# Splitting feed-forward weights into two parts with casting and adding DMAs instead of ScalarE and VectorE

## The chip, the cores and the metric

The kernel runs on one core of a Trainium2 chip. The time is the device time of one execution in microseconds (us); the figure quoted for a kernel is the median of its runs. The kernel before took 936.67 us (3 runs, 936.47 to 938.75). Engines are named as in the profile: PE is TensorE's matmul, PEld its weight load, DVE is VectorE, ACT is ScalarE, POOL is GpSimd, SP is SyncE, which here only issues DMAs.

## What is computed

One decoder layer on x of 512 tokens by 1024 columns in float32. Three token mixers (a gated recurrence, a differential attention and a forgetting attention) are merged and added to x; then comes the feed-forward part, which the change touches:

```python
h = rmsnorm(x, norm2_g[l])
u = causal_dwconv(h @ ffn_up[l], ffn_conv_w[l], ffn_conv_b[l])   # ffn_up: 1024 x 5632
u_gate, u_val = jnp.split(u, 2, axis=-1)
x = x + (jax.nn.gelu(u_gate) * u_val) @ ffn_down[l]              # ffn_down: 2816 x 1024
return rmsnorm(x, final_g)
```

## The kernel before

Every large matmul is made of three: each float32 operand is split into a high part of type float32r and a low part, operand minus high part, and the products high x high, high x low and low x high are summed in PSUM.

A weight block is 128 x 1024 numbers, 512 KB. `load_w` (L93) fetches one: SP issues a DMA into a tile `wr` (L100), ACT casts `wr` into the high tile `wh` (L101), DVE subtracts and writes the low tile `wl` (L102). `wr`, `wh` and `wl` have three buffers each, in rotation: a block's tiles are those of the block three before. `load_wp` (L105) does the same into four half-size tiles of another pool (`wph`, `wpl`).

The feed-forward part has two stages. In the up stage 44 blocks of `ffn_up` are used in turn, one item each: 24 matmuls of 512 columns into one PSUM bank (`up`, L912), 16 that read `wh` and then 8 that read `wl`. The first three items are done together in halves of 256 columns (`up_half`, L917), block 0 from `load_wp`, blocks 1 and 2 from `load_w`. After each second item `glu` (L921) runs the convolution and the gate on ACT and DVE and leaves `acth` and `actl`. The down stage does the 512 columns of either half of the output (`hf` 0 and 1) one after the other: 11 blocks each, 24 matmuls a block into four banks `psd` (`dmm`, L971), in which `wh` and `wl` alternate. The last 2 (`hf` 0) and 4 (`hf` 1) blocks of a half come from `load_wp` and are "held": all of a bank's matmuls are then done bank by bank. For `hf` 0 the blocks before these are called d0 to d8 here, for `hf` 1 e0 to e6.

The order on each engine is not written out by hand: a scheduler orders the instructions by its own simulated times and by which buffers are free. Each engine then works through its list in order; whatever waits on a semaphore holds all that stands behind it on that engine.

Of the kernel before, what the change touches and what calls it, by code (L numbers as in the profile page):

```python
# [10 lines left out]
F32 = mybir.dt.float32  # L11
F32R = mybir.dt.float32r
AF = mybir.ActivationFunctionType
ALU = mybir.AluOpType
ADD, SUB, MUL, MAX = ALU.add, ALU.subtract, ALU.mult, ALU.max
# [6 lines left out]
NF = DFF // 128  # L22
# [5 lines left out]
WCOL = 1088  # L28
# [18 lines left out]
def build(ctx, tc, A, out):  # L47
    nc = tc.nc
    PE, V, SC, G = nc.tensor, nc.vector, nc.scalar, nc.gpsimd
# [3 lines left out]
    wpool = ctx.enter_context(tc.tile_pool(name="wpool", bufs=3))  # L53
# [7 lines left out]
    def pg(name, dt=F32):  # L61
        return page.tile([128, 512], dt, name=name, tag="pg")
# [4 lines left out]
    def bank(name):  # L67
        return psm.tile([128, 512], F32, name=name, tag="mm")

    def abank(name):  # L70
        return psa.tile([128, 512], F32, name=name, tag="at")
# [4 lines left out]
    def mm(ps, a, b, start, stop):  # L76
        PE.matmul(ps, a, b, start=start, stop=stop)  # L77

    def mm3(ps, pairs, late=0):


        hh = [((ah, bh), (ah, bl), (al, bh)) for ah, al, bh, bl in pairs]
        if late == 2:
            seq = [m for t in hh for m in t]
        else:
            seq = [t[i] for t in hh for i in ((0, 1) if late == 0 else (0, 2))]
            seq += [t[2 if late == 0 else 1] for t in hh]
        for j, (a, b) in enumerate(seq):
            mm(ps, a, b, j == 0, j == len(seq) - 1)
# [3 lines left out]
    def load_w(ap, n, parts=1):  # L93
        raw = wpool.tile([128, WCOL], F32, name="wr", tag="wr")
        hi = wpool.tile([128, WCOL], F32R, name="wh", tag="wh", bufs=3)
        lo = wpool.tile([128, WCOL], F32R, name="wl", tag="wl", bufs=3)
        with tc.high_priority() if hp[0] else ExitStack():
            for p in range(parts):
                c = slice(n // parts * p, n // parts * (p + 1))
                nc.sync.dma_start(raw[:, c], ap[:, c])  # L100
                SC.copy(hi[:, c], raw[:, c])  # L101
                V.tensor_sub(lo[:, c], raw[:, c], hi[:, c])  # L102
        return hi, lo

    def load_wp(ap):  # L105

        raw = wpool.tile([128, WCOL], F32, name="wr", tag="wr")
        nc.sync.dma_start(raw[:, :1024], ap)
        res = []
        for p in range(2):  # L110
            c = slice(512 * p, 512 * (p + 1))
            h = pg("wph", F32R)
            l = pg("wpl", F32R)
            SC.copy(h, raw[:, c])
            V.tensor_sub(l, raw[:, c], h)
            res.append((h, l))
        return res
# [72 lines left out]
    for w in range(KD // 2):  # L190
        load_x(2 * w)
        hi, lo = load_w(A["wv_d"][w], 1024, 2)
        load_x(2 * w + 1)
        if w == 0:
            nc.sync.dma_start(cols[:, 8:], A["cols"][:, 8:])
        todo = [(t, 2 * w + kk, j) for kk in range(2) for j in range(3) for t in range(NT)]
        if w == KD // 2 - 1:
            todo.sort()
        for t, k, j in todo:
            kk = k % 2  # L200
            a, b = ((xh[k], hi), (xl[k], hi), (xh[k], lo))[j]
            mm(pst[t], a[:, 128 * t:128 * (t + 1)], b[:, 512 * kk:512 * (kk + 1)],
               k == 0 and j == 0, k == KD - 1 and j == 2)

    ss1 = const.tile([128, 2, NT], F32, name="ss1")
    for t in range(NT):
        for hf in range(2):
            xt = ag("xt")
            nc.sync.dma_start(xt, A["x"][128 * t:128 * (t + 1), 512 * hf:512 * (hf + 1)])
            SC.activation(xt, xt, AF.Square, accum_out=ss1[:, hf, t:t + 1])  # L210
    pre_w = [load_w(A["w_t"][i], 1024) for i in (T_DQ, T_DK)]
    ssum = small([128, NT], "ssum", 1)
    V.tensor_add(ssum, ss1[:, 0, :], ss1[:, 1, :])
# [47 lines left out]
    def vload_t(ap, kper, n):  # L261
        return lambda: [load_w(ap[0], kper * n), load_w(ap[1], kper * n)]
# [582 lines left out]
        hp[0] = True  # L845
    hp[0] = False

    def up_w(idx, paged=False):
        if paged:
            pp = load_wp(A["up_t"][idx])  # L850
            return lambda k: tuple(x[:, 128 * (k % 4):128 * (k % 4 + 1)] for x in pp[k // 4])
        hi, lo = load_w(A["up_t"][idx], 1024)
        return lambda k: (hi[:, 128 * k:128 * (k + 1)], lo[:, 128 * k:128 * (k + 1)])

    first_w = {0: up_w(0, True)}
    x1 = []
    x1p = [[pg("x1") for _ in range(2)] for _ in range(NT)]
# [12 lines left out]
    for t in range(NT):  # L870
# [3 lines left out]
        for hf in range(2):  # L874
            ps = bank("pswo")
# [36 lines left out]
    def up(wt, name):  # L912
        ps = bank(name)
        mm3(ps, [wt(k) + (h2h[k], h2l[k]) for k in range(KD)])
        return ps

    def up_half(ps, wt, hf):  # L917
        c = slice(256 * hf, 256 * (hf + 1))
        mm3(ps[:, c], [wt(k) + (h2h[k][:, c], h2l[k][:, c]) for k in range(KD)])

    def glu(c, psg, psv):  # L921
        ug = conv(psg, [col("fw", 44 * j + c) for j in range(3)], col("fb", c))
        uv = conv(psv, [fwh[:, 22 * j + c:22 * j + c + 1] for j in range(3)], fwh[:, 66 + c:67 + c])
        q = pg("gq")
        SC.activation(q, ug, AF.Square)
        V.tensor_scalar(q, q, GELU_A, 1.0, op0=MUL, op1=ADD)
        V.tensor_mul(q, q, ug)
        SC.activation(q, q, AF.Tanh, scale=GELU_C)  # L928
        V.scalar_tensor_tensor(ug, q, 1.0, ug, op0=ADD, op1=MUL)  # L929
        V.tensor_mul(ug, ug, uv)  # L930
        acts.append(split(ug, "act", ag if c < 10 else None))

    acts = []
    order = [i for c in range(NF) for i in (c, NF + c)]
    first_w[1] = up_w(order[1])
    first_w[2] = up_w(order[2])
    pss = [bank("psu") for _ in range(3)]
    for hf in range(2):
        for n in range(3):
            up_half(pss[n], first_w[n], hf)  # L940
    nxt = up_w(order[3])
    glu(0, pss[0], pss[1])
    prev = pss[2]
    for n in range(3, 2 * NF):
        w, nxt = nxt, up_w(order[n + 1]) if n + 1 < 2 * NF else None
        ps = up(w, "psu")
        if n % 2:
            glu(n // 2, prev, ps)
        prev = ps

    ss3 = const.tile([128, NT, 2], F32, name="ss3")
    NP = NF // 2
# [6 lines left out]
    def finish(t):  # L959
        z = rsqrt_act(ss3[:, t, 1:2], ss3[:, t, 0:1], "rs3")  # L960
        o = [pg("of") for _ in range(2)]
        SC.activation(o[1], x1[t][1], AF.Copy, scale=z)
        V.tensor_scalar(o[0], x1[t][0], z, None, op0=MUL)
        nc.sync.dma_start(out[128 * t:128 * (t + 1), 0:512], o[0])
        SC.dma_start(out[128 * t:128 * (t + 1), 512:1024], o[1])

    for hf in range(2):
        pst = [bank("psd") for _ in range(NT)]
        held = []

        def dmm(t, k, wh, wl):  # L971
            ts_ = slice(128 * t, 128 * (t + 1))
            ah, al = acts[k]
            for j, (a, b) in enumerate(((al, wh), (ah, wl), (ah, wh))):
                mm(pst[t], a[:, ts_], b, k == 0 and j == 0, k == NF - 1 and j == 2)

        nl = NLAST[hf]
        nxt = load_w(A["dn_t"][hf, 0], 1024)
        for p in range(NP - nl):
            hi, lo = nxt  # L980
            if p + 1 < NP - nl:
                nxt = load_w(A["dn_t"][hf, p + 1], 1024)
            else:
                held = [(p, load_wp(A["dn_t"][hf, p])) for p in range(NP - nl, NP)]
            for kk in range(2):
                for t in range(NT):
                    dmm(t, 2 * p + kk, hi[:, 512 * kk:512 * (kk + 1)], lo[:, 512 * kk:512 * (kk + 1)])
        for t in range(NT):
            xx = x1[t][hf]
            for p, w in held:  # L990
                for kk in range(2):
                    dmm(t, 2 * p + kk, *w[kk])
            V.tensor_add(xx, pst[t], xx)
            SC.activation(abank("sqj"), xx, AF.Square, accum_out=ss3[:, t, hf:hf + 1])
            xg = pg("xg")
            V.tensor_mul(xg, xx, fgp[hf])
            x1[t][hf] = xg
            if not hf:
                V.tensor_scalar(ss3[:, t, 0:1], ss3[:, t, 0:1], 1.0 / D, EPS, op0=MUL, op1=ADD)
            else:  # L1000
                finish(t)
# [67 lines left out]
```

## Time and profile before

| | |
|---|---|
| median of 3 runs | 936.67 us |
| the profiled execution | 938.8 us |
| its span, first to last instruction | 937.0 us |
| PE busy | 925.1 us, 99% |
| DVE, ACT, POOL busy | 633.8, 482.7, 95.9 us |
| bytes moved by DMA | 95.14 MB, mean 102 GB/s |
| TensorE's granted clock, mean | 0.998 |

The span is that of the profiled execution; 1.8 us of its time lie outside it. PE's busy time says that hardly any moment lacks a matmul. Idle time of the other engines costs nothing as long as PE finds its operands ready. For a change in how weights arrive, the parts to read are the chain of work that ended last, what PE waits for in the feed-forward stages, and how long before its use a block is ready.

### The profile page before, as it was taken

Reading aid. Unit: us, or ns where it says so; the run is one execution under the profiler, and the core shown is the slowest. Engines: PE = TensorE matmul, PEld = TensorE weight load, DVE = VectorE, ACT = ScalarE, POOL = GpSimd, SP = SyncE. Lnnn points to the kernel's source line nnn. Section 1 sums busy time; section 2 is a strip of 40 time slices with the busy share of each in tenths; the row PEclk is TensorE's granted clock in tenths of the full one; section 3 lists DMA queues with packets and bytes.
Section 4 is the critical chain, followed back from the end, with each engine's and each line's share of the span. In section 5 each row is a group of like instructions: output and inputs, shape, how many; then the busy total and the mean of one; then the engine's idle time right before and its main releaser. Section 6 shows DMA issues by size and latency. Waiting matters only on the chain.

```text
span 937.0 us, 11825 instructions
## 1 busy us (share of the span) xinstructions
PE 925.1 (99%) x4363; PEld 771.6 (82%) x4363; DVE 633.8 (68%) x1215; ACT 482.7 (52%) x835; POOL 95.9 (10%) x77
## 2 busy tenths in 40 slices
PE   9999999999999999999999999999999999999997
PEld 6788888998887887888888889888888888888885
DVE  5679797787759778857656734877777777633323
ACT  7577777755465657444454434554444454422212
POOL 0021310200121126321100000000000000000000
PEclk9999999999999999999999999999999999999999
DMA  9522222222322221322245510322322322334112
GB/s 328 173 93 96 80 90 69 69 91 91 107 85 84 97 96 57 105 98 97 73 142 167 189 43 1 113 90 91 111 90 91 111 91 91 113 103 144 45 68 90
DMA packets 31577, 95.14 MB, mean 102 GB/s; under 512 B 3824, under 2 KB 5364, under 8 KB 31520
## 3 DMA queue, kind: packets, MB, share of 16 engines
q1 hardware_dynamic: 30944, 93.35, 29.4%
q10 hardware_dynamic: 576, 1.05, 0.3%
q8 instruction: 34, 0.56, 0.2%
q14 instruction: 23, 0.19, 0.1%
HBM read 92.26 MB, written 2.12 MB: 101 GB/s over the span
## 4 chain that ended last, share of the span: by engine, by line
PE 96%; DVE 2%; issue 1%; ACT 0%; DMA 0%; POOLq 0%; POOL 0%; SPq 0%; ACTq 0%
PE psu L77 26%; PE psgt L77 14%; PE psd L77 12%; PE psbr L77 9%; PE psg L77 6%; PE psv L77 5%; PE psk L77 5%; PE psx L77 5%; PE pswo L77 5%; PE psq L77 4%; PE pss L77 2%; PE pso L77 2%; PE pst L431 1%; DVE wl L102 0%; PE psh L891 0%
## 5 line engine op out<-in xcount | busy, mean ns | idle before, releaser
L102 DVE TENSOR_TENSOR wl<-wr,wh 128x1024 fp32r<-128x1024 f32 (+2 forms) x143 | 175.2, 1225 | 77.4 <-ACT wh L101 62.0
L101 ACT CAST wh<-wr 128x1024 fp32r<-128x1024 f32 (+2 forms) x143 | 146.8, 1028 | 151.3 <-PE psu L77 51.7
L77 PE MATMUL psu<-h2h,wh 128*128 128x512 f32 (+1 forms) x360 | 135.6, 380 | 0.0
L77 PE MATMUL psu<-h2l,wh 128*128 128x512 f32 (+1 forms) x360 | 135.5, 380 | 0.0
L77 PE MATMUL psu<-h2h,wl 128*128 128x512 f32 (+1 forms) x360 | 85.7, 380 | 0.0
L77 PEld LDWEIGHTS psu<-h2l,wh 128*128 128x128 f32 x360 | 67.7, 188 | 12.8
L77 PEld LDWEIGHTS psu<-h2h,wh 128*128 128x128 f32 x360 | 67.7, 188 | 12.7
L77 PEld LDWEIGHTS psu<-h2h,wl 128*128 128x128 f32 x360 | 65.8, 188 | 12.8
L77 PE MATMUL psgt<-xh,wh 128*128 128x512 f32 x192 | 75.6, 394 | 0.0
L77 PE MATMUL psgt<-xl,wh 128*128 128x512 f32 x192 | 75.6, 394 | 0.0
L77 PE MATMUL psd<-wl,acth 128*128 128x512 f32 x128 | 49.8, 389 | 0.0
L77 PE MATMUL psd<-wh,actl 128*128 128x512 f32 x128 | 49.6, 389 | 0.0
L77 PE MATMUL psd<-wh,acth 128*128 128x512 f32 x128 | 49.5, 389 | 0.0
L77 PE MATMUL psgt<-xh,wl 128*128 128x512 f32 x192 | 48.3, 390 | 0.0
L77 PEld LDWEIGHTS psgt<-xh,wh 128*128 128x128 f32 x192 | 36.1, 188 | 7.3
L77 PEld LDWEIGHTS psgt<-xl,wh 128*128 128x128 f32 x192 | 36.1, 188 | 7.2
L77 PEld LDWEIGHTS psgt<-xh,wl 128*128 128x128 f32 x192 | 35.8, 188 | 7.4
L867 POOL TENSOR_TENSOR rs3y<-rs3y,mhalf 128x1 f32<-128x1 f32 x4 | 2.2, 549 | 358.7 <-DVE rs3y L866 358.7
L929 DVE SCALAR_TENSOR_TENSOR u<-gq,u 128x512 f32<-128x512 f32 x22 | 15.2, 692 | 33.2 <-ACT gq L928 33.2
L909 DVE SCALAR_TENSOR_TENSOR u<-psu,cols,u 128x511 f32<-128x511 f32 (+1 forms) x44 | 32.9, 748 | 6.1 <-ACT u L906 5.4
L123 ACT CAST acth<-u 128x512 fp32r<-128x512 f32 x22 | 13.7, 621 | 43.8 <-DVE u L930 43.8
L437 ACT CAST wth<-pst 128x512 fp32r<-128x512 f32 (+3 forms) x48 | 19.6, 423 | 28.8 <-PE pst L431 27.1
(287 smaller groups left out, 2160.9 us busy)
## 6 DMA issues: line engine op xcount, KB each, us to landing
wr<-w_t_in SPq DMA_DIRECT2D x56, 512.0 KB, 3.2
wr<-up_t_in SPq DMA_DIRECT2D x44, 512.0 KB, 3.2
wr<-dn_t_in SPq DMA_DIRECT2D x22, 512.0 KB, 3.2
wr<-br_r_in SPq DMA_DIRECT2D x8, 512.0 KB, 3.2
wr<-w_out_in SPq DMA_DIRECT2D x8, 512.0 KB, 4.0
xraw<-xT_in SPq DMA_DIRECT2D x8, 256.0 KB, 5.2
wr<-wv_d_in SPq DMA_DIRECT2D x8, 256.0 KB, 5.6
xt<-x_in SPq DMA_DIRECT2D x8, 256.0 KB, 5.2
```

Of the source, the lines that this page charges most:

```text
L77: PE.matmul(ps, a, b, start=start, stop=stop)
L101: SC.copy(hi[:, c], raw[:, c])
L102: V.tensor_sub(lo[:, c], raw[:, c], hi[:, c])
L123: SC.copy(h, src)
L431: PE.transpose(ps[:, 128 * i:128 * (i + 1)], ws[i][:, 128 * j:128 * (j + 1)], ident)
L437: SC.copy(h[:, 128 * j:], ps[:, 128 * j:])
L867: G.tensor_tensor(y, y, mhalf[:, 0:1], op=ALU.pow)
L909: V.scalar_tensor_tensor(u[:, s:], ps[:, :512 - s], w[j], u[:, s:], op0=MUL, op1=ADD)
L929: V.scalar_tensor_tensor(ug, q, 1.0, ug, op0=ADD, op1=MUL)
```

## The change

A new function `load_wd` fetches a block in another way. POOL issues a DMA straight from the weights in memory into `wh`, which casts to float32r on the way. ACT writes the negative of `wh` into `wl` (an activation Copy with scale -1). POOL issues a second DMA of the same weights into `wl`, which adds what it brings to what is there, so `wl` ends as weight minus high part. There is no `wr` tile, no cast on ACT and no subtraction on DVE. The 41 up blocks from the fourth on and the 16 down blocks that are not held (9 and 7) use it. Blocks are asked for two items ahead in the program, not one; the tiles keep three buffers.

```diff
+    def load_wd(ap, n):
+
+
+        hi = wpool.tile([128, WCOL], F32R, name="wh", tag="wh", bufs=3)
+        lo = wpool.tile([128, WCOL], F32R, name="wl", tag="wl", bufs=3)
+        c = slice(0, n)
+        G.dma_start(hi[:, c], ap)
+        SC.activation(lo[:, c], hi[:, c].bitcast(F32), AF.Copy, scale=-1.0)
+        G.dma_start(lo[:, c], ap, accum_op=ADD)
+        return hi, lo
...
-    def up_w(idx, paged=False):
+    def up_w(idx, paged=False, load=load_wd):
...
-        hi, lo = load_w(A["up_t"][idx], 1024)
+        hi, lo = load(A["up_t"][idx], 1024)
...
-    first_w[1] = up_w(order[1])
-    first_w[2] = up_w(order[2])
+    first_w[1] = up_w(order[1], load=load_w)
+    first_w[2] = up_w(order[2], load=load_w)
...
-    nxt = up_w(order[3])
+    nxt = [up_w(order[3])]
...
-        w, nxt = nxt, up_w(order[n + 1]) if n + 1 < 2 * NF else None
-        ps = up(w, "psu")
+        for i in range(n + len(nxt), min(n + 3, 2 * NF)):
+            nxt.append(up_w(order[i]))
+        ps = up(nxt.pop(0), "psu")
...
-        nxt = load_w(A["dn_t"][hf, 0], 1024)
+        nxt = []
         for p in range(NP - nl):
-            hi, lo = nxt
-            if p + 1 < NP - nl:
-                nxt = load_w(A["dn_t"][hf, p + 1], 1024)
-            else:
+            for i in range(p + len(nxt), min(p + 3, NP - nl)):
+                nxt.append(load_wd(A["dn_t"][hf, i], 1024))
+            hi, lo = nxt.pop(0)
+            if p + 1 == NP - nl:
                 held = [(p, load_wp(A["dn_t"][hf, p])) for p in range(NP - nl, NP)]
```

In the changed file L101, L102 and L77 keep their numbers; in `load_wd` L111 is the casting DMA, L112 the negation and L113 the adding DMA. The program's order is the same on every engine until the last matmuls of the output projection, shortly before the feed-forward part.

POOL at the passage from the up to the down stage, after the change; `wh_7521` and `wl_7522` are d0's tiles, 7526 and 7527 d1's, 7531 and 7532 d2's, 7560 and 7561 d3's, 7589 and 7590 d4's, 7618 and 7619 d5's:

```order
L111 DMA wh_7521<-dn_t_in 128x1024
L111 DMA wh_7526<-dn_t_in 128x1024
L113 DMA wl_7522<-dn_t_in 128x1024
L113 DMA wl_7527<-dn_t_in 128x1024
L111 DMA wh_7531<-dn_t_in 128x1024
L113 DMA wl_7532<-dn_t_in 128x1024
L111 DMA wh_7560<-dn_t_in 128x1024
L111 DMA wh_7589<-dn_t_in 128x1024
L113 DMA wl_7561<-dn_t_in 128x1024
L111 DMA wh_7618<-dn_t_in 128x1024
L113 DMA wl_7590<-dn_t_in 128x1024
L113 DMA wl_7619<-dn_t_in 128x1024
```

Before, POOL had between the norm ahead of the up stage and the final norm nothing but these, the small powers of the two norms:

```order
L867 TENSOR_TENSOR rs2y_5576<-rs2y_5576,mhalf_78 128x1
L867 TENSOR_TENSOR rs2y_5667<-rs2y_5667,mhalf_78 128x1
L867 TENSOR_TENSOR rs3y_8207<-rs3y_8207,mhalf_78 128x1
L867 TENSOR_TENSOR rs3y_8245<-rs3y_8245,mhalf_78 128x1
L867 TENSOR_TENSOR rs3y_8283<-rs3y_8283,mhalf_78 128x1
```

All 114 DMAs of the 57 blocks have come onto POOL's list; the adding DMA of d3 stands behind the casting DMA of d4, and that of d4 behind the casting DMA of d5.

ACT at the same passage, before (7599 is d2's tile, 7629 d3's, 7659 d4's, 7689 d5's):

```order
L101 CAST wh_7599<-wr_7598 128x1024
L906 ACTIVATE u_7538<-psu_7509,fwh_5700 128x512
L925 ACTIVATE gq_7542<-u_7534 128x512
L928 ACTIVATE gq_7542<-gq_7542 128x512
L123 CAST acth_7549<-u_7534 128x512
L101 CAST wh_7629<-wr_7628 128x1024
L101 CAST wh_7659<-wr_7658 128x1024
L101 CAST wh_7689<-wr_7688 128x1024
```

and after:

```order
L112 ACTIVATE wl_7532<-wh_7531 128x1024
L939 ACTIVATE gq_7501<-gq_7501 128x512
L134 CAST acth_7508<-u_7493 128x512
L125 CAST wph_7760<-wr_7758 128x512
L125 CAST wph_7764<-wr_7758 128x512
L125 CAST wph_7770<-wr_7768 128x512
L125 CAST wph_7774<-wr_7768 128x512
L112 ACTIVATE wl_7561<-wh_7560 128x1024
L112 ACTIVATE wl_7590<-wh_7589 128x1024
L112 ACTIVATE wl_7619<-wh_7618 128x1024
```

In the place of each cast stands the negation, now between two DMAs; the casts of the held blocks have moved ahead of d3's.

PE where d2's matmuls end and d3's begin, before (d3 is 7629 and 7630):

```order
L77 MATMUL psd_7561<-wh_7599,acth_6259 128x512
L77 MATMUL psd_7558<-wh_7629,actl_6341 128x512
L77 MATMUL psd_7558<-wl_7630,acth_6340 128x512
L77 MATMUL psd_7558<-wh_7629,acth_6340 128x512
L77 MATMUL psd_7559<-wh_7629,actl_6341 128x512
```

and after (7560 and 7561):

```order
L77 MATMUL psd_7520<-wh_7531,acth_6254 128x512
L77 MATMUL psd_7517<-wh_7560,actl_6334 128x512
L77 MATMUL psd_7518<-wh_7560,actl_6334 128x512
L77 MATMUL psd_7519<-wh_7560,actl_6334 128x512
L77 MATMUL psd_7520<-wh_7560,actl_6334 128x512
L77 MATMUL psd_7517<-wl_7561,acth_6333 128x512
```

The first matmul that reads a low tile has moved from the second to the fifth place of its block. Counted from the first matmul of the down stage, d3's low tile is first read by the 77th, d0's high tile last by the 38th and d1's by the 48th (before, by the 40th and the 48th).

## Rows read from the trace of the kernel before

**Rows 1.** Page, header and part 1: busy time of the engines

```profile
span 937.0 us, 11825 instructions
PE 925.1 (99%) x4363; PEld 771.6 (82%) x4363; DVE 633.8 (68%) x1215; ACT 482.7 (52%) x835; POOL 95.9 (10%) x77
```

**Rows 2.** Chain that ended last, from 560 us: start, us, what

```profile
576.07 234.82 PE psu L77 x1082
810.89 114.25 PE psd L77 x504
...
925.16 0.70 DVE x L993
...
927.49 4.85 issue
```

**Rows 3.** What PE waited for, whole span: total us, times, longest

```profile
PE psbr L77 <- ACT yrh L686: 2.2, 1, 2.2
PE pwarm L170 <- POOL warm L167: 1.3, 1, 1.3
PE pso L77 <- DVE wtl L438: 0.8, 1, 0.8
PE pst L431 <- DVE mx L535: 0.5, 1, 0.5
PE psv L77 <- ACT wh L101: 0.5, 1, 0.5
```

**Rows 4.** Chain over the whole span, one item of 24 matmuls: start, us

```profile
88.02 5.44 PE psg L77 x24
```

**Rows 5.** Instructions by form, 560 to 937 us: busy, mean ns, idle before

```profile
L102 DVE TENSOR_TENSOR wl<-wr,wh 128x1024 fp32r<-128x1024 f32 x56 | 68.5, 1223 | 55.4 <-ACT wh L101 49.0 <-PE psu L77 5.0 <-ACT gq L928 0.8
L101 ACT CAST wh<-wr 128x1024 fp32r<-128x1024 f32 x56 | 59.0, 1054 | 91.6 <-PE psu L77 51.7 <-PE psd L77 34.0 <-issue 5.2
```

**Rows 6.** PE in order of time at the down stage's start and d0's last use

```profile
810.72 0.39 PE L77 MATMUL psd<-wh,actl 128*128 128x512 f32 x1
810.95 0.39 PE L77 MATMUL psd<-wl,acth 128*128 128x512 f32 x1
...
819.56 0.39 PE L77 MATMUL psd<-wh,acth 128*128 128x512 f32 x1
```

**Rows 7.** ACT and then DVE in order of time, casts and subtractions of d2 to d4

```profile
809.11 1.06 ACT L101 CAST wh<-wr 128x1024 fp32r<-128x1024 f32 x1
...
819.99 1.05 ACT L101 CAST wh<-wr 128x1024 fp32r<-128x1024 f32 x1 [2.76 <-PE psd L77]
821.80 1.05 ACT L101 CAST wh<-wr 128x1024 fp32r<-128x1024 f32 x1 [0.76 <-PE psd L77]
...
821.08 1.23 DVE L102 TENSOR_TENSOR wl<-wr,wh 128x1024 fp32r<-128x1024 f32 x1 [3.12 <-ACT wh L101]
```

**Rows 8.** Line L100's DMAs, 569 to 811 us: issue ns min/median/max, then landing

```profile
L100 SPq DMA_DIRECT2D wr<-up_t_in x37: 327/328/328, 587.3 to 779.6; - x37
...
DMA to landing us min/median/max: 3.0/3.2/5.0
```

**Rows 9.** The same line, 811 to 937 us

```profile
L100 SPq DMA_DIRECT2D wr<-dn_t_in x11: 327/328/328, 812.2 to 879.7; - x11
...
DMA to landing us min/median/max: 3.1/3.5/4.4
```

**Rows 10.** The same line, 0 to 30 us

```profile
DMA to landing us min/median/max: 3.3/5.4/7.3
```

**Rows 11.** Stretches: length, PE, PEld, DVE, ACT, POOL busy, PEclk, DMA share, GB/s

```profile
0.00:30.00 30.00, 28.17 (x105) 20.95 (x106) 17.68 (x53) 21.24 (x41) 2.22 (x9) 1.00 0.82 296
...
690.00:811.00 121.00, 121.00 (x536) 100.19 (x535) 89.03 (x123) 58.17 (x79) 0.00 (x0) 1.00 0.29 96
```

**Rows 12.** DMA queues and issues, 690 to 811 us: packets, MB, share of 16 engines

```profile
q1 hardware_dynamic: 3192, 11.57, 28.8%
...
wr<-up_t_in SPq DMA_DIRECT2D x17, 512.0 KB, 3.2
wr<-dn_t_in SPq DMA_DIRECT2D x5, 512.0 KB, 3.2
```

**Rows 13.** POOL's instructions by line, whole span

```profile
L867 POOL TENSOR_TENSOR rs3y<-rs3y,mhalf 128x1 f32<-128x1 f32 x4 | 2.2, 549 | 358.7 <-DVE rs3y L866 358.7
```

## The prediction

> **What bounds the kernel now.** I read the page's header and part 1 first: PE is busy for 925.1 of 937.0 us [rows 1], so only time in which PE has nothing to do can be won, and any new wait of PE is lost in full. Then the chain that ended last: from 576 us on it is one unbroken run of up-stage matmuls, 234.82 us, and one of down-stage matmuls, 114.25 us, and only the last 12 us are something else [rows 2]. Then PE's waits: the five longest, 5.3 us together, all lie ahead of the feed-forward part; the only one for a weight is 0.5 us [rows 3]. So the stages that the change touches run at PE's own pace, one item of 24 matmuls in 5.44 us, 0.227 us a matmul [rows 4]. The 62 us that DVE waits for the casts, and the casts for PE's buffers [rows 5], are waits of engines with time to spare. What counts is how early a block's tiles are ready, and the down stage shows that best [rows 6, 7]: d0's high tile is last read at 819.56 + 0.39 = 819.95 us, d3's cast into it begins at 819.99, its low tile is done at 821.08 + 1.23 = 822.31. PE reads that tile first with the 74th matmul of the stage, at 810.72 + 73 x 0.227 = 827.3. Spare: 5.0 us. The raw block had long been there, because it lands in a buffer of its own.
>
> **What goes and what comes.** 57 blocks change over (41 up, 16 down). DVE loses 57 subtractions of 1.223 us, 69.7 us; ACT's 57 casts of 1.054 us become 57 negations of the same shape, which I take at the same 1.05 us [rows 5]; SP loses 57 DMAs. None of it is on PE's path, so it gives nothing back: 0. POOL gets 114 DMAs. It is otherwise idle in these stages but for the powers of the final norm, 0.55 us each [rows 13], which stand behind the last of them on POOL and run after the held blocks, when all are through: 0.
>
> What does move the time is the chain behind a free buffer. Before, a free tile needed a cast and a subtraction, 1.05 + 1.22 us. Now it needs a casting DMA, the negation, and an adding DMA, one after the other; the first can't start before PE has let the high tile go, so the look-ahead of two items doesn't help beyond what three buffers allow. With four handovers of 0.04 us (819.95 to 819.99, [rows 6, 7]) rounded up to 0.2, the two DMAs must fit into the window less 1.25 us:
> - Up stage: the high tile goes free after 16 of 24 matmuls (15 x 0.227 + 0.39 = 3.79 us into the item three before), the low tile is needed 16 matmuls into its own item: 3 x 5.44 + 3.63 - 3.79 = 16.2, less 1.25 leaves 14.9 us for two DMAs.
> - d3: d0's high tile is free after the 38th matmul, 37 x 0.227 + 0.39 = 8.78 us into the stage; its low tile is read by the 77th, at 76 x 0.227 = 17.23. Left: 7.2 us.
> - e3, counted in the same way (29th matmul, 6.74 us, and the 77th): 9.2 us.
> - The other down blocks: free at the end of the block three before, needed four matmuls into their own, 2 x 5.44 + 0.91 - 0.16 - 1.25 = 10.4 us.
> - POOL's order adds one limit: d4's adding DMA stands behind d5's casting DMA, which waits for d2's last matmul (16.49 us); d4's low tile is read at 22.67. So issue plus adding DMA must be under 6.2 us.
>
> **The price of the two DMAs.** The trace has no DMA from POOL, none that casts or adds. Nearest is the same block fetched by SP: 0.33 us to issue, landing 3.0 us at best and 3.2 in the median in the up stage [rows 8], 3.5 and at most 4.4 in the down stage [rows 9]. The other end is the start of the kernel, where the engines are 82% busy [rows 11]: median 5.4, at most 7.3 [rows 10]. How full would they be? 22 blocks take 28.8% of 121 us [rows 11, 12], 1.58 us of all 16 engines each. Two per item are 3.2 of 5.44 us, 58%; if the adding one takes twice as long, since it reads its destination too, 4.7, 87%. So I take the casting DMA at 4.4, the slowest of a plain one in that stage, and the adding one at 5.4, the median of the stretch that is as full: 9.8 us together. POOL's issue I take at 0.55, its shortest row with a wait ahead [rows 13]. Ends: 3.2 + 3.2 and 7.3 + 7.3.
>
> The Trainium skill (DMA: Bandwidth & Descriptors, Latency and other measured facts) puts the first byte of a DMA from GpSimd at about 1 us and from SP at about 0.6; by it the sum would be 2 x 3.6 = 7.2 us, which just fits d3, and nothing would be lost. The Trainium skill (Collectives: The Full Stack, The bandwidth ceiling) says that an add in the DMA path is free in itself but needs two source reads; by it the adding DMA takes 1.6 us longer, 8.0 us in all, and d3 waits 0.8. No row here shows either.
>
> **The sum.** At 9.8 us: the up stage has 5.1 us to spare; d3 waits 9.8 - 7.2 = 2.6 us; e3 0.6; the others fit by 0.6, d4 by 0.2. PE loses 3.2 us. On the profiled execution's 938.8 us that is 942.0; that execution was 2.1 us above the median of its runs, so on the median, 936.67 + 3.2 = **939.9 us**. At the low end no block waits. At the high end d3 loses 7.4, d4 1.7, and each later one 14.6 - 10.4 = 4.2 less what the block before it lost: 2.5, 1.7, 2.5, 1.7; then e3 5.4, e5 4.2: 27 us, 963.8; the up stage still fits by 0.3. The case's own range is 936.7 to 964.
>
> **Rivals.** *Hidden* (not slower): both DMAs land within some 7 us and no block is late, or by under 2.8 us in all. For it: the plain landing of 3.2 to 3.5, and 5 us of slack now. Against: the window of d3 leaves 0.8 us over two plain DMAs. Time 936.7.
>
> *The DMA engines become the bound.* If casting and adding each take the engines twice as long as a plain copy, an item needs 4 x 1.58 = 6.3 us, more than PE's 5.44. Then no look-ahead helps and each of the 57 items waits 0.88 us: +50 us, 987. It decides as soon as an item's two DMAs need more than 5.44 us, 3.4 times one plain copy. For it: nothing shows what the two kinds take. Against: it needs both to be slow.
>
> *Faster*: PE gains from emptier engines. For it: 70 us less on DVE. Against: PE has no wait in these stages to give back [rows 2, 3], and the 12 us at the end have no weights in them. It needs the 2.8 us that can be told from no change, 933.
>
> If the cast should copy the bits without rounding, the low part is zero and the same instructions take the same time: no case of its own.
>
> **How the numbers follow.** Down-stage waits 0.42; hidden 0.36; DMA-bound 0.17; faster 0.05. About 0.3%, 2.8 us, is what can be told from no change. So faster 0.05, same 0.36, slower 0.59. The range takes in the whole of the first two and the beginning of the DMA-bound case, where an item needs some 0.65 us too much: 936 to 975; left out are most of that case and most of faster, 0.18.
>
> **What would show it.** Right: PE's waits name the down stage's first `wl` of a block, the longest for d3, the next for e3, and the up stage's run of matmuls is still about 235 us long; ACT's negations wait for DMAs. POOL's two DMAs, from issue to landing, should add to 9 to 11 us. Wrong towards hidden: the sum is under 7.2 and the down run stays unbroken. Wrong towards the DMA bound: PE waits in most up items and the DMA share is over 0.9 from 590 us on. The forecast fails as well if POOL takes far longer than 0.55 us to issue, since each issue also holds the DMAs behind it.

## The result and the profile after

The changed kernel took 1005.43 us in the median of 4 runs (1002.29 to 1011.49), the kernel before 936.57 beside it (4 runs, 935.18 to 938.75): a ratio of 1.0749 [1.0729, 1.0768] (the brackets hold the 95% interval, here and below), 68.9 us slower. The forecast was 939.9 us, range 936 to 975; the sign was right, the size far off. The profiled execution took 1002.29 us.

Header and first part of the page after, as [rows 1]:

```profile
span 1000.5 us, 11829 instructions
PE 943.0 (94%) x4363; PEld 777.1 (78%) x4363; DVE 571.0 (57%) x1158; ACT 479.2 (48%) x835; POOL 180.2 (18%) x191
```

The span is 63.5 us longer. PE has the same 4363 matmuls but is busy 17.9 us longer, and nearly all the rest are waits, 45.5 us: what PE waited for, as [rows 3] (us in total, times, longest):

```profile
PE psu L77 <- DMA wl<-up_t_in: 27.7, 14, 2.8
PE psd L77 <- DMA wl<-dn_t_in: 17.8, 7, 4.5
```

Both are low tiles that an adding DMA had not finished. Where in the span it went, by the start of the down stage (PE in order of time), and the entry of the chain that answers to the first of [rows 2], the same 6.39 us into the stage:

```profile
850.75 0.61 PE L77 MATMUL psd<-wh,actl 128*128 128x512 f32 x2
```

```profile
574.10 17.23 PE psu L77 x122
```

From that point to the down stage it was 810.72 - 576.07 = 234.7 us before [rows 2, 6] and is now 850.75 - 574.10 = 276.7: the up stage, which the forecast called safe by 5.1 us, lost 42.0. What follows lost 23.5. (The up stage began 2.0 us earlier; 42.0 + 23.5 - 2.0 = 63.5.)

What POOL, which now issues all these DMAs, waited for (us in total, times, longest):

```profile
POOL wl L113 <- ACT wl L112: 260.6, 53, 9.4
...
POOL wh L111 <- PE psd L77: 22.2, 8, 9.1
POOL wh L111 <- PE psu L77: 15.8, 4, 13.1
```

A casting DMA in the up stage waits for PE to free its tile 4 times, 15.8 us. An adding DMA waits for its negation 53 times out of 57, 260.6 us. So the buffers don't set when a block's chain starts; POOL's list does. One round of two blocks, all engines in order of time (start, length; in brackets the idle time before and who ended it):

```profile
748.68 0.87 POOL L113 DMA_DIRECT2D wl<-up_t_in  x1 [3.36 <-ACT wl L112]
...
749.22 1.61 POOL L111 DMA_DIRECT2D wh<-up_t_in  x2
757.28 1.06 ACT L112 ACTIVATE wl<-wh 128x1024 fp32r<-128x1024 f32 x1 [7.57 <-DMA wh<-up_t_in]
758.25 0.61 ACT L939 ACTIVATE gq<-gq 128x512 f32<-128x512 f32 x1
758.65 0.88 POOL L113 DMA_DIRECT2D wl<-up_t_in  x1 [7.82 <-ACT wl L112]
...
760.35 0.62 ACT L134 CAST acth<-u 128x512 fp32r<-128x512 f32 x1 [1.49 <-DVE u L941]
760.88 0.77 ACT L917 ACTIVATE u<-psu,cols 128x512 f32<-128x512 f32 x1
...
761.55 1.04 ACT L112 ACTIVATE wl<-wh 128x1024 fp32r<-128x1024 f32 x1
...
762.89 0.88 POOL L113 DMA_DIRECT2D wl<-up_t_in  x1 [3.36 <-ACT wl L112]
...
763.45 1.60 POOL L111 DMA_DIRECT2D wh<-up_t_in  x2
764.09 0.67 PE L77 MATMUL psu<-h2h,wl 128*128 128x512 f32 x1 [2.84 <-DMA wl<-up_t_in]
```

Read it as a ring. Right behind one block's adding DMA (748.68) POOL issues two casting DMAs. The three are in flight together, and ACT gets the first high tile only at 757.28, 8.60 us later. The second negation stands on ACT behind the gate's tanh, a wait for DVE, a cast and the convolution's first step, which reads a PSUM bank: it starts 4.27 us after the first. It and the handover take 1.34 us more, and only then does POOL come to the second adding DMA (762.89), behind which the next two casting DMAs stand. Sum: 14.21 us for two blocks that PE could use up in 2 x 5.44 = 10.88.

This round is the longest of its kind; from 736 us on they take 12.4 to 14.2 us, and before that a round holds three blocks. For the mean, the fourth and the last of the up stage's 41 adding DMAs:

```profile
597.61 0.87 POOL L113 DMA_DIRECT2D wl<-up_t_in  x1 [5.97 <-ACT wl L112]
...
840.53 0.86 POOL L113 DMA_DIRECT2D wl<-up_t_in  x1 [3.36 <-ACT wl L112]
```

Between them are 37 blocks in 242.92 us, 6.57 us a block or 13.1 for two. PE's pace would be 37 x 5.44 = 201.3, and the difference, 41.6 us, is nearly all of the up stage's loss of 42.0.

The DMA engines are not full on the average: 0.63 and 0.71 in two stretches of the up stage, as [rows 11].

```profile
570.00:690.00 120.00, 111.04 (x527) 92.62 (x527) 53.27 (x87) 46.53 (x68) 24.93 (x35) 0.96 0.63 144
690.00:811.00 121.00, 107.33 (x450) 85.52 (x450) 53.39 (x82) 47.58 (x65) 27.74 (x37) 0.97 0.71 162
```

Within a stretch they are, by turns. The tenths of the time that they were busy, in 40 slices of the 29 us from 748 to 777:

```profile
DMA  9409799999920010469991968999996000879950
```

A burst fills them, then they stand empty until ACT and POOL have passed the ring once more. The share of them that the new DMAs took over the whole span (queue: packets, MB, share), as [rows 12]:

```profile
q0 software_dynamic: 16416, 59.78, 26.4%
```

That is 264.1 us of all 16 engines for 57 blocks, 4.63 us a block, 85% of an item of 5.44. The forecast's estimate was 4.7 and 87%. Landing after the issue, in the median, as [rows 8, 9]:

```profile
wh<-up_t_in POOLq DMA_DIRECT2D x41, 512.0 KB, 6.5
wl<-up_t_in POOLq DMA_DIRECT2D x41, 512.0 KB, 5.4
wh<-dn_t_in POOLq DMA_DIRECT2D x16, 512.0 KB, 6.1
wl<-dn_t_in POOLq DMA_DIRECT2D x16, 512.0 KB, 5.4
```

### The profile page after: what moved, and what is told of

It is laid out like the page before. It is cut to its first block, busy times and chain, and to the rows that moved or that the text cites. A ratio compares the mean times of both kernels' runs of the same rounds, so it can differ in the third digit from the quotient of the medians.

```text
span 1000.5 us, 11829 instructions
## 1 busy us (share of the span) xinstructions
PE 943.0 (94%) x4363; PEld 777.1 (78%) x4363; DVE 571.0 (57%) x1158; ACT 479.2 (48%) x835; POOL 180.2 (18%) x191
## 3 DMA queue, kind: packets, MB, share of 16 engines
q1 hardware_dynamic: 22736, 63.46, 18.9%
q10 hardware_dynamic: 576, 1.05, 0.3%
## 4 chain that ended last, share of the span: by engine, by line
PE 61%; issue 26%; POOL 7%; DMA 3%; DVE 2%; ACT 1%; POOLq 0%; SPq 0%; ACTq 0%
PE psgt L77 13%; PE psbr L77 8%; PE psg L77 5%; PE psv L77 5%; PE psk L77 4%; PE psx L77 4%; PE pswo L77 4%; PE psq L77 4%; PE psu L77 4%; POOL wh L111 3%; PE psd L77 3%; POOL wl L113 3%; PE pss L77 2%; PE pso L77 2%; PE pst L442 1%
## 5 line engine op out<-in xcount | busy, mean ns | idle before, releaser
L112 ACT ACTIVATE wl<-wh 128x1024 fp32r<-128x1024 f32 x57 | 60.3, 1057 | 203.0 <-DMA wh<-up_t_in 127.0
L77 PE MATMUL psu<-h2h,wh 128*128 128x512 f32 (+1 forms) x360 | 137.1, 384 | 0.0
L77 PE MATMUL psu<-h2l,wh 128*128 128x512 f32 (+1 forms) x360 | 136.6, 383 | 0.0
L77 PE MATMUL psu<-h2h,wl 128*128 128x512 f32 (+1 forms) x360 | 95.4, 410 | 27.7 <-DMA wl<-up_t_in 27.7
L102 DVE TENSOR_TENSOR wl<-wr,wh 128x1024 fp32r<-128x1024 f32 (+2 forms) x86 | 106.3, 1236 | 24.1 <-ACT wh L101 15.3
L101 ACT CAST wh<-wr 128x1024 fp32r<-128x1024 f32 (+2 forms) x86 | 86.7, 1010 | 59.9 <-issue 16.0
L77 PEld LDWEIGHTS psu<-h2h,wl 128*128 128x128 f32 x360 | 69.1, 201 | 47.8 <-DMA wl<-up_t_in 34.4
L77 PEld LDWEIGHTS psu<-h2h,wh 128*128 128x128 f32 x360 | 68.9, 192 | 13.9 <-issue 0.4
L77 PEld LDWEIGHTS psu<-h2l,wh 128*128 128x128 f32 x360 | 68.4, 190 | 13.3
L77 PE MATMUL psgt<-xh,wh 128*128 128x512 f32 x192 | 75.6, 394 | 0.0
L77 PE MATMUL psgt<-xl,wh 128*128 128x512 f32 x192 | 75.6, 394 | 0.0
L113 POOL DMA_DIRECT2D wl<-up_t_in x41 | 35.9, 875 | 204.9 <-ACT wl L112 192.6
L77 PE MATMUL psd<-wl,acth 128*128 128x512 f32 x128 | 52.4, 409 | 17.8 <-DMA wl<-dn_t_in 17.8
L1005 DVE TENSOR_TENSOR x<-psd,x 128x512 f32<-128x512 f32 x8 | 5.5, 690 | 104.0 <-PE psd L77 104.0
L920 DVE SCALAR_TENSOR_TENSOR u<-psu,fwh,u 128x511 f32<-128x511 f32 (+1 forms) x44 | 32.8, 746 | 33.2 <-ACT u L917 32.4
L77 PE MATMUL psd<-wh,acth 128*128 128x512 f32 x128 | 51.2, 404 | 0.0
L77 PE MATMUL psgt<-xh,wl 128*128 128x512 f32 x192 | 48.3, 390 | 0.0
L111 POOL DMA_DIRECT2D wh<-up_t_in x41 | 32.4, 911 | 81.8 <-DVE z L680 65.7
L77 PEld LDWEIGHTS psd<-wl,acth 128*128 128x128 f32 x128 | 25.0, 196 | 26.3 <-DMA wl<-dn_t_in 21.1
L77 PE MATMUL psd<-wh,actl 128*128 128x512 f32 x128 | 44.9, 392 | 0.0
L77 PEld LDWEIGHTS psgt<-xh,wh 128*128 128x128 f32 x192 | 36.1, 188 | 7.3
```

Source lines behind the costliest of these rows:

```text
L111: G.dma_start(hi[:, c], ap)
L112: SC.activation(lo[:, c], hi[:, c].bitcast(F32), AF.Copy, scale=-1.0)
L113: G.dma_start(lo[:, c], ap, accum_op=ADD)
L920: V.scalar_tensor_tensor(u[:, s:], ps[:, :512 - s], w[j], u[:, s:], op0=MUL, op1=ADD)
```

## The experiments

Two theories. *Chain*: POOL's and ACT's in-order lists tie the DMAs into the ring above. *Engines*: casting and adding DMAs load the DMA engines so much that the time is lost in any order. The ratios are to the kernel before, run on the same chip.

**Only the casting DMA.**

```diff
-        SC.activation(lo[:, c], hi[:, c].bitcast(F32), AF.Copy, scale=-1.0)
-        G.dma_start(lo[:, c], ap, accum_op=ADD)
+        raw = wpool.tile([128, WCOL], F32, name="wr", tag="wr")
+        nc.sync.dma_start(raw[:, c], ap)
+        V.tensor_sub(lo[:, c], raw[:, c], hi[:, c])
```

> The high tile comes by the casting DMA on POOL, the low tile by the old way: SP fetches the raw block, DVE subtracts. No negation, no adding DMA, 57 DMAs on POOL. Theory 'chain' (POOL's and ACT's in-order lists couple the DMAs: a casting DMA stands behind an adding DMA that waits for a negation that waits on ACT): with nothing on POOL that waits for ACT the chain is gone; 936 to 940 us, PE waits in the feed-forward part under 2 us. Rival 'engines' (casting and adding DMAs cost the DMA engines too much): a casting DMA plus a plain one still need 2.3 + 1.6 of 5.44 us, so about the same if the adding kind is to blame, but 960 or more, with waits on wh, if the casting kind is.

Measured: 937.98 us, 1.0027 [1.0015, 1.0039]; no wait of PE for a weight. As expected by *chain*. The queue of POOL's DMAs:

```profile
q0 software_dynamic: 8208, 29.89, 9.7%
```

9.7% of 938.3 us over 57 blocks is 1.60 us a casting DMA, what a plain one takes (1.58 by [rows 11, 12]).

**Only the adding DMA.**

```diff
-        G.dma_start(hi[:, c], ap)
+        raw = wpool.tile([128, WCOL], F32, name="wr", tag="wr")
+        nc.sync.dma_start(raw[:, c], ap)
+        SC.copy(hi[:, c], raw[:, c])
```

> The high tile comes by the old way (SP fetches the raw block, ACT casts), ACT writes the negative, POOL's adding DMA completes the low tile. No casting DMA, 57 DMAs on POOL. 'Chain': the next block's work no longer stands behind the adding DMA, only one POOL DMA per item: 936 to 942 us, waits of PE under 4 us, although ACT has 57 casts more. 'Engines': if the adding kind is to blame, 970 to 1005 us with waits on wl in most items.

Measured: 939.28 us, 1.0033 [1.0017, 1.005]. Its queue of POOL's DMAs, and then the up stage in two stretches (length, busy PE, PEld, DVE, ACT, POOL, granted clock, DMA share, GB/s):

```profile
q0 software_dynamic: 8208, 29.89, 18.9%
```

```profile
570.00:690.00 120.00, 120.00 (x586) 101.68 (x585) 63.89 (x104) 77.71 (x103) 17.56 (x21) 1.00 0.75 179
690.00:810.00 120.00, 120.00 (x531) 99.37 (x530) 65.23 (x100) 78.39 (x99) 19.30 (x23) 1.00 0.83 196
```

An adding DMA takes 18.9% of 935.7 us over 57, 3.10 us, twice a plain one. It landed in 6.4 us in the up stage, later than in the changed kernel, at a DMA share of 0.75 to 0.83, and yet PE never stood still there; its only wait for a weight, 1.1 us, is in the down stage. A slow adding DMA alone costs hardly anything.

**The second DMA without the add.**

```diff
-        G.dma_start(lo[:, c], ap, accum_op=ADD)
+        G.dma_start(lo[:, c], ap)
```

> The second DMA overwrites the low tile with the cast block in place of adding, so the low part is not weight minus high part; the order, the waits and the number of DMAs are as after the change. 'Chain': the negation is still waited for; only what the add itself costs goes: 990 to 1005 us. 'Engines' with the adding kind to blame: the wait goes, 940 to 965 us.

Measured: 940.2 us, 1.0053 [1.0031, 1.0076]. *Chain* as I had put it expected 990 to 1005 and missed; the result lies at the lower edge of what *engines* expected. POOL's list is the same as the changed kernel's in all 114 places. POOL still waited for negations, but with two DMAs that landed in 4.3 and 3.8 us the round fitted:

```profile
POOL wl L113 <- ACT wl L112: 169.8, 49, 8.8
POOL wh L111 <- PE psu L77: 80.3, 19, 13.1
```

Now it was PE that POOL waited for in 19 blocks. So the ties are not enough by themselves, and by the run before neither is the adding DMA; a ring as tight as this costs nothing while it turns faster than PE. That each of the two is needed is what the next runs had to show from the other side.

**The negation on DVE.**

```diff
-        SC.activation(lo[:, c], hi[:, c].bitcast(F32), AF.Copy, scale=-1.0)
+        V.tensor_scalar(lo[:, c], hi[:, c].bitcast(F32), -1.0, None, op0=MUL)
```

> All as after the change, but DVE writes the negative in place of ACT. 'Chain': the negations no longer stand 3.3 us apart behind GLU work on ACT, so POOL's cycle for two items falls from 12.7 to 14.2 us towards 11: 945 to 975 us. 'Engines': same DMAs, same time, 1000 to 1010 us.

Measured: 970.22 us, 1.0371 [1.0354, 1.0388]: half of the loss goes, at the same load (q0 26.7%), where *engines* expected no difference. How much of this is the place behind the gate's work on ACT the run doesn't show: on DVE the negation is also shorter (0.70 us against 1.06), and POOL's list differs in 44 of its 114 places.

**One item ahead in place of two.**

```diff
-        for i in range(n + len(nxt), min(n + 3, 2 * NF)):
+        for i in range(n + len(nxt), min(n + 2, 2 * NF)):
...
-            for i in range(p + len(nxt), min(p + 3, NP - nl)):
+            for i in range(p + len(nxt), min(p + 2, NP - nl)):
```

> As after the change, but blocks are asked for one item ahead in the program, not two. 'Chain': a casting DMA starts no earlier than POOL's list lets it, so what counts is how the scheduler interleaves the two kinds, not the look-ahead; 985 to 1025 us. 'Engines': the same DMAs, 1000 to 1010 us. If the look-ahead of two itself did the harm (casting DMAs issued in pairs, which land late), 940 to 970 us.

Measured: 1011.87 us, 1.0802 [1.0755, 1.0849]. The scheduler gave POOL the same list as in the changed kernel, in all 114 places, so the casting DMAs still go in pairs. The run is in effect a repetition: it shows that the look-ahead written in the program doesn't reach POOL here, but tests neither the pairs nor the two theories.

**Only the up blocks; only the down blocks.** In the first `load_wd` becomes `load_w` in the down stage, in the second in `up_w`.

```diff
-                nxt.append(load_wd(A["dn_t"][hf, i], 1024))
+                nxt.append(load_w(A["dn_t"][hf, i], 1024))
```

```diff
-    def up_w(idx, paged=False, load=load_wd):
+    def up_w(idx, paged=False, load=load_w):
```

> Only the 41 up blocks come in the new way, the 16 down blocks as before. Both theories: the loss of the up stage alone, 42 us by the stages' lengths in the two traces (283.1 against 241.0 us): 975 to 985 us.

> Only the 16 down blocks come in the new way, the 41 up blocks as before. 'Chain': the down stage starts with full buffers, waits as d3, e3 and the others did, 15 to 23 us: 952 to 960 us. The prediction's own sum for this stage, 3.2 us, would give 940.

Measured: 979.95 us (1.0472 [1.0446, 1.0497]) and 956.82 us (1.0223 [1.0207, 1.0238]). The up stage costs 43.6 us, the down stage 20.5; together 64.1 of 68.9. (The kernel before had 936.36 us beside them.) Of the second, PE's busy time, its waits for these weights, and two of the seven (in order of time):

```profile
PE 930.4 (97%) x4363; PEld 773.4 (81%) x4363; DVE 613.4 (64%) x1199; ACT 482.7 (50%) x835; POOL 118.0 (12%) x109
```

```profile
PE psd L77 <- DMA wl<-dn_t_in: 13.9, 7, 3.2
```

```profile
832.88 0.76 PE L77 MATMUL psd<-wl,acth 128*128 128x512 f32 x1 [3.23 <-DMA wl<-dn_t_in]
...
902.74 0.50 PE L77 MATMUL psd<-wl,acth 128*128 128x512 f32 x1 [2.08 <-DMA wl<-dn_t_in]
```

By their place in the stage they are the low tiles of d3 and e3; the other five are those of d1 (1.73), d2 (1.03), d7 (1.39), d8 (2.42) and e6 (2.03).

**POOL's list in a fixed order, in both stages.** The adding DMA is traced one block later, and each DMA is queued behind the one traced before it (order alone, no wait).

```diff
+    plate, plast = [], [None]
+    pone = lambda r: nc.cur_bb.bb.instructions[-1]
...
-        G.dma_start(hi[:, c], ap)
+        with tc.issue_after(plast[0]) if plast[0] is not None else ExitStack():
+            plast[0] = pone(G.dma_start(hi[:, c], ap))
...
-        G.dma_start(lo[:, c], ap, accum_op=ADD)
+        plate.append((lo[:, c], ap))
+        if len(plate) > 1:
+            add_late()
...
+    def add_late():
+        lo, ap = plate.pop(0)
+        with tc.issue_after(plast[0]):
+            plast[0] = pone(G.dma_start(lo, ap, accum_op=ADD))
...
+        if n == 2 * NF - 2:
+            add_late()
...
+            if p == NP - nl - 2:
+                add_late()
```

> The same 114 DMAs, negations and waits as after the change; only POOL's list is put in a fixed order, each adding DMA behind the casting DMA of the next block (wh of n+1, wl of n, wh of n+2, wl of n+1). 'Chain': by the time POOL comes to an adding DMA its negation is done, and no casting DMA waits for an adding DMA that waits for ACT; a PE item of 5.44 us is longer than POOL's two issues (1.8 us) and than the engines' 4.6 us, so 937 to 950 us. 'Engines' (the adding DMA, which takes the DMA engines 3.0 to 3.1 us against 1.6 of a plain or casting one, costs the time by itself): 4.6 of 5.44 us in every order, so 980 to 1005 us.

Measured: 964.45 us, 1.03 [1.0284, 1.0317], outside what either theory expected. By stage it is plain. PE's waits, then POOL's (here L113 is the casting DMA, L114 the negation, L123 the adding DMA):

```profile
PE psd L77 <- DMA wl<-dn_t_in: 18.3, 6, 6.0
...
PE psu L77 <- DMA wl<-up_t_in: 1.4, 1, 1.4
```

```profile
POOL wh L113 <- PE psu L77: 134.3, 38, 13.3
...
POOL wh L113 <- PE psd L77: 73.9, 13, 16.0
...
POOL wl L123 <- ACT wl L114: 55.4, 33, 5.1
```

In the up stage the waits fell from 27.7 us to 1.4 by order alone; there a casting DMA now waits for PE, as the forecast had assumed. The two DMAs landed no sooner (5.2 + 7.4 us in the median against 6.5 + 5.4). Nor did ACT's list get easier: from 736 us on it repeats the same seven instructions as in the changed kernel, and the second negation still starts 4.27 us after the first:

```profile
736.86 1.06 ACT L114 ACTIVATE wl<-wh 128x1024 fp32r<-128x1024 f32 x1 [2.44 <-DMA wh<-up_t_in]
...
741.13 1.06 ACT L114 ACTIVATE wl<-wh 128x1024 fp32r<-128x1024 f32 x1
```

The DMA engines worked off the same DMAs without the holes (slices from 736 to 765 us), and in the stretches their share is higher, not lower:

```profile
DMA  7999999898698257899997978989995999987989
```

```profile
570.00:690.00 120.00, 118.62 (x581) 100.37 (x580) 61.61 (x100) 56.27 (x80) 29.17 (x41) 1.00 0.82 176
690.00:810.00 120.00, 119.75 (x529) 98.80 (x527) 62.97 (x97) 55.33 (x76) 31.39 (x44) 1.00 0.89 194
```

That ends *engines* for the up stage. The down stage lost more than in the changed kernel, since there the fixed order itself is bad: an adding DMA stands behind a casting DMA that waits for the end of the block two before, and from there only 5.44 + 0.91 - 0.16 - 0.04 = 6.15 us are left for an issue of 0.55 and a landing of 7.3, 1.7 us too few; three of the six waits are 1.83, 1.97 and 2.19 (the others, 2.81, 3.47 and 6.00, are longer).

**The fixed order in the up stage, the down blocks as before.** The last diff with, in the down stage, `load_w`.

> The 41 up blocks come by casting and adding DMAs in the fixed order (each adding DMA behind the casting DMA of the next block), the 16 down blocks as before the change. 'Chain': in the run with the fixed order in both stages PE waited 1.4 us in the up stage and 18.3 in the down stage, so 936 to 940 us here. 'Engines': 41 blocks at 4.6 us of the DMA engines each cost as in the run with only the up blocks changed, 970 to 980 us.

Measured: 937.76 us, 1.0013 [1.0004, 1.0023]. 41 of the 57 blocks with the same three steps cost 1.3 us, against 43.6 in the scheduler's order.

**Six high tiles in the down stage.** Only the down blocks changed, and in `load_wd`:

```diff
+    turn = [0]
...
-        hi = wpool.tile([128, WCOL], F32R, name="wh", tag="wh", bufs=3)
+        turn[0] += 1
+        tag = "wr" if turn[0] % 2 else "wh"
+        hi = wpool.tile([128, WCOL], F32R, name="wh", tag=tag, bufs=3)
```

> Only the 16 down blocks come in the new way, and their high tiles take turns in the buffers of wh and wr, six in all in place of three (wr is hardly used in this stage). The DMAs are the same. Theory 'window': a down block's casting DMA must wait for PE to finish the block three before, and 11.6 us later its low tile is needed, while casting, negating and adding take some 5.9 + 1.1 + 0.9 + 5.2 = 13 us; with six high tiles the casting is out of this window and 7 us are left in it, which fit: 936 to 941 us. Rival 'engines': same DMAs, same 957 us.

Measured: 936.24 us, 1.0003 [0.9991, 1.0014]. The 20.5 us are gone with the same DMAs, which *engines* can't explain. But POOL's list came out in another order too, one casting DMA and one adding DMA in turn, with the casting ones further ahead. So this run alone doesn't tell whether the buffers or the order did it; the next one does for the fixed order.

**Both: the fixed order and six high tiles; and six high tiles alone.** The diffs are those of the fixed order and of the six high tiles, on the changed kernel.

> All 57 blocks in the new way, the fixed order on POOL, and six high tiles in place of three. 'Chain' and 'window' together: the up stage fits by the order, the down stage by the buffers: 936 to 943 us. 'Engines': 4.6 us of DMA engines per block as ever, 960 us or more.

> As after the change, with six high tiles in place of three and the scheduler's own order, which then puts one casting DMA and one adding DMA in turn on POOL, the casting ones two to three blocks ahead. 'Chain': a negation then never waits long for its casting DMA and no adding DMA holds a casting DMA that is needed soon: 936 to 945 us. 'Engines': 980 us or more.

Measured: 936.68 us, 1.0001 [0.9992, 1.0011], and 939.04 us, 1.0036 [1.0022, 1.005]. Of the first, page, POOL's longest wait (L117 is the negation, L126 the adding DMA) and stretches:

```profile
PE 923.3 (99%) x4363; PEld 770.1 (82%) x4363; DVE 569.3 (61%) x1158; ACT 479.0 (51%) x835; POOL 176.6 (19%) x191
```

```profile
POOL wl L126 <- ACT wl L117: 229.7, 53, 11.6
```

```profile
690.00:811.00 121.00, 121.00 (x535) 100.21 (x534) 66.23 (x102) 57.68 (x79) 31.30 (x44) 1.00 0.84 194
811.00:872.00 61.00, 61.00 (x271) 50.49 (x270) 11.60 (x21) 15.68 (x23) 14.25 (x20) 1.00 0.82 200
```

All 57 blocks by casting and adding DMAs, DVE at 569.3 us, and PE without a wait for a weight: no loss. POOL's list is the same in all 114 places as with the fixed order and three high tiles (964.45 us), so it was not the order on POOL but the buffers that took away the waits of the down stage, 18.3 us there: the window between PE's last use of a tile and its first use three blocks later. POOL's adding DMAs wait for negations nearly as long as in the changed kernel (260.6 us), so these waits alone aren't the loss. No gain either; no version beat the kernel before, since PE had nothing to give back. With six high tiles alone the scheduler takes another order (one casting DMA and one adding DMA in turn), so that run changes two things at once.

## Why the prediction was wrong

- **The failed step: "Up stage: ... leaves 14.9 us for two DMAs", "5.1 us to spare".** That window starts when PE lets the high tile go. It holds only if POOL is at the casting DMA by then; what stands ahead of it on POOL and ACT was put at nothing. POOL came to it late: casting DMAs of the up stage waited for PE 15.8 us in 4 cases, adding DMAs for ACT 260.6 us in 53. I took POOL's order into the sum for d4 alone ("POOL's order adds one limit"), and not for the up items. What I should have summed is one round of POOL's list with ACT's work in it: 13.1 us in the mean for two blocks against 10.88. This is 43.6 us of 68.9, and the fixed order in the up stage, with DMAs that landed no sooner (5.0 + 7.1 us against 6.5 + 5.4), took all but 1.3 of it away.
- **The prices of the two DMAs** were too low where they stand in a burst. I took 4.4 + 5.4 = 9.8 us; in the changed kernel the medians are 6.5 + 5.4 in the up stage and 6.1 + 5.4 in the down stage. The casting DMA is the one that I mis-sized: alone on POOL's queue it landed in 3.9 us (up, casting only), but behind an adding DMA and beside a second casting one it lands later. The adding one was right, and so was the load of the engines. In the up stage the price alone would have done no harm: 6.5 + 5.4 = 11.9 us fit into 14.9.
- **The down stage** was right in kind for the two blocks that the sum had waiting. With only the down blocks changed, d3 waited 3.23 us (predicted 2.6) and e3 2.08 (0.6). For d3 that run shows the chain: the casting DMA issued at 820.02, the negation at 826.06 (6.04), the adding DMA at 827.42, PE at 832.88 (5.46). With that run's landings, 5.9 + 5.2 = 11.1 us, the windows of 7.2 and 9.2 would have given 3.9 and 1.9, so here it was the price that was mis-sized. d1, d2, d7, d8 and e6, 8.6 of the 13.9 us, weren't in the sum; their casting DMAs stood right behind an adding DMA on POOL, with no idle time between (802.86, 810.91, 845.24, 853.35 and 908.78), so POOL's list had a part there as well. In the changed kernel itself d3 was the worst again (4.50), but e3, which was to be the next, came sixth of seven (1.77), behind e6 (3.56) and d0 (2.92). Six high tiles confirmed the window where POOL's order was held fixed.
- **A term that was missing: PE's clock after a wait.** PE was busy 17.9 us longer for the same matmuls. Two groups of 8 equal matmuls of the changed kernel, and then stretches of it:

```profile
764.09 3.65 PE L77 MATMUL psu<-h2h,wl 128*128 128x512 f32 x8 [2.84 <-DMA wl<-up_t_in]
...
771.26 1.98 PE L77 MATMUL psu<-h2h,wl 128*128 128x512 f32 x8
```

```profile
764.00:766.00 2.00, 1.91 (x5) 1.54 (x6) 1.65 (x4) 0.00 (x0) 1.04 (x2) 0.57 0.82 98
768.00:772.00 4.00, 4.00 (x19) 3.27 (x19) 0.39 (x1) 1.58 (x2) 0.63 (x1) 1.00 0.62 225
```

  After 2.84 us without work the granted clock was 0.57, near the lower of its two levels (1.2 of 2.4 GHz), and 8 matmuls took 1.67 us more. Over the run that is 17.9 / 45.5 = 0.39 us for each us waited (by stage, from the losses above, (42.0 - 27.7) / 27.7 = 0.52 in the up stage and (23.5 - 17.8) / 17.8 = 0.32 after it); with only the down blocks it is (930.4 - 925.1) / 13.9 = 0.38. No experiment took the clock apart from the waits; this part is read from rows.
- **The rivals.** "The DMA engines become the bound" gave 987, the nearest number, by a false mechanism: its condition, 3.4 plain copies an item, wasn't met (4.63 / 1.58 = 2.9), the DMA share was 0.63 and 0.71 in the changed kernel's up stage, and at 0.82 to 0.89 in the fixed order PE waited only 1.4 us. "Hidden" is what the kernel does once order and buffers allow it. The negation cost 1.057 us, as taken (1.05). The Trainium skill (Collectives: The Full Stack, The bandwidth ceiling) says of the reduce step of a collective that its add needs two source reads; for the adding DMA here the trace agrees in size, 3.10 us of the engines against 1.60. The sum had reckoned with twice the time too, but it was the sum of the wrong window.
- **A reading that was off**, without weight in the sum: the 62 us that DVE waits for casts are those of the whole span. In the feed-forward part they are 49.0 [rows 5].

What stays open: how the loss in the ring divides between the second negation's place on ACT and the burst of three DMAs. Moving the negation to DVE gave back 35.2 us, but it shortened the negation and changed POOL's order too, and in the fixed order the same place on ACT cost next to nothing. Open as well is how the down stage's 20.5 us divide between the window and POOL's list in the scheduler's order.

## What to carry to other kernels

When a step becomes DMA, compute, DMA on one in-order queue, add up one full round of that queue, with the other engine's list in it, and hold it against the consumer's pace; slack counted from buffer release is worth only what the queue lets through. Here a mean DMA share of 0.7 with holes in its fine slices was the sign of such a ring rather than of a lack of bandwidth; put the dependent DMA behind the next block's independent one, where the buffers allow it. And price a wait of PE above its length: here each us cost some 0.3 to 0.5 more.

## What the runs showed of the hardware

- For a block of 512 KB a casting DMA from POOL takes the DMA engines as long as a plain one (1.60 against 1.58 us of all 16), an adding one twice that (3.10).
- POOL's record of the issue of a casting DMA took 0.53 us when its list held no adding DMAs (row below, of the run with only casting DMAs; ns, min/median/max), that of an adding DMA 0.87 us. Records that stand next to each other overlap, though: the casting DMA behind the adding one of 748.68 started 0.54 us after it, at 749.22.

```profile
L111 POOL DMA_DIRECT2D wh<-up_t_in x40: 527/528/572, 585.3 to 792.9; - x40
```

- At a DMA share of 0.82 to 0.89 over 240 us (the fixed order's up stage) PE waited for a weight only once, 1.4 us.
